# Seven half-size products for the down projection of a SwiGLU half step

## The chip, the cores and the metric

The kernel runs on one core of one Trainium2 chip. The metric is the device time of a whole execution in microseconds; the kernel before takes 1567.97 us (median of three runs, 1567.06 to 1568.4). All data is float32.

## The reference

One layer of a diffusion backbone works on 640 tokens (512 latent, 128 context) of width 1024. It has three parts, each with a modulated RMSNorm ahead of it and a gated residual addition behind it:

```python
def swiglu(h, w_gate, w_up, w_down):
    return (jax.nn.silu(h @ w_gate) * (h @ w_up)) @ w_down

h = modulate(rms_norm(x, norm_ffn1), sh1, sc1)
x = x + 0.5 * gt1 * swiglu(h, w_ffn1_gate, w_ffn1_up, w_ffn1_down)   # first half step
...                                                                  # mixer: Fourier branch and gated linear attention
h = modulate(rms_norm(x, norm_ffn2), sh3, sc3)
x = x + 0.5 * gt3 * swiglu(h, w_ffn2_gate, w_ffn2_up, w_ffn2_down)   # second half step
```

The feed-forward width is 2816, so gate and up map 1024 to 2816 and down maps 2816 back to 1024. The modulation vectors come from a product with `w_ada`, which is streamed in during the first half step.

## The kernel before, in words

**Layout.** Activations stand transposed, with features on the 128 partitions and the 640 tokens along the free axis, cut into two halves of 320 (NH). The 1024 features are 8 tiles of 128, the 2816 hidden features 22 tiles. A "page" is a buffer of 128 x 2 x 640 floats; 26 of them (NPAGES) rotate for everything. Raw weights arrive in two buffers `wraw`, their split copies live in 10 blocks `wspl` (NBLK) of 128 x 2 x 512.

**Precision by splitting.** A float32 value is written as hi + lo, both fp32r: `split` (L105) lets ScalarE copy hi (L107) and VectorE compute lo = src - hi (L108), which reads two operands from SBUF. Every product is then three matmuls: hi*hi, hi*lo, lo*hi.

**Seven products.** `Pair7` (L457) computes two output tiles of 128 features for all 640 tokens as a 2 x 2 block product with seven half-size products in place of eight. With n = 4 inner tiles a product is 4 x 3 = 12 matmuls of 128 x 320 columns, a pair 84. GpSimd forms four sums of the weights in place (L474, L477, L481, L485), all seven weight blocks are split, and class `Take` combines the seven results from PSUM on VectorE (L530 to L545, one ScalarE copy at L529). The sums of the activations are made once, by `Act7`. The products of a pair run in the order 1, 2, 7, 4, 6, 5, 3.

**A half step** (`ffn`, L570). Hidden tiles come in couples f, f+1: a gate pair, then an up pair. `TakeUp.done` multiplies silu(gate) and up on GpSimd (L566, 128 x 640) and splits the result into one page per tile. The 22 tiles are handled in PARTS (4, 6, 6, 6). The down product of a part runs one gate pair late, between the gate and the up pair of the next part: `down` (L587) takes one output tile at a time with plain three-matmul products (L138), 8 x nf x 3 x 2 matmuls for nf hidden tiles, and adds them into X (L372). The last part goes through `halved` (L376): first all eight output tiles for one half of the tokens, then for the other, nf x 3 matmuls each (L392), added to X at L397. While the second half runs, the norm of the first half is already built (first half step: `Norm.add` L319 to L323, `stats` L329, `apply` L355 to L365) or the output is transposed and scaled (second half step: L1267 to L1286). The second half step cuts the tokens at 384 there.

**Start of a half step.** Tiles 0 and 1 are computed with plain products, while `Act7` builds the sums. The order on each engine in that stretch is written out: `pin(m1)` fixes it from `m1 = mark()` on.

**Order.** Outside pinned stretches a planner fixes one order per engine: in its own timing of the program an instruction is placed when its inputs and buffers are there, the earlier line first. At run time each engine's queue, SP's with the weight and `w_ada` loads included, is worked off in that order.

Of the kernel before, what the change touches and what calls it, by code (L numbers as in the profile page):

```python
# [8 lines left out]
F32R = mybir.dt.float32r  # L9
# [6 lines left out]
KD = 8  # L16
# [9 lines left out]
C_F, C_Q, C_K, C_V, C_R, C_A, C_G = 0, 512, 1024, 1536, 2560, 3584, 3616  # L26
NPAGES = 26
NBLK = 10
M1, M2 = 2, 4
PARTS = (4, 6, 6, 6)  # L30


@with_exitstack
def trunk_kernel(ctx: ExitStack, tc: tile.TileContext, I, O):
# [34 lines left out]
    def page(dt=F32):  # L69
        uid[0] += 1  # L70
        return pgs.tile([P, 2, N], dt, tag="pg", name=f"pg{uid[0]}")
# [13 lines left out]
    def out_ps():  # L85
        return [pb_ps(), pb_ps()] if "pb" in ppool else mm_ps()
# [12 lines left out]
    def load(w, r0, nk, c0, cols):  # L99
        uid[0] += 1  # L100
        raw = wraw.tile([P, 2048], F32, tag="wraw", name=f"wraw{uid[0]}")
        v = raw[:, 0:nk * cols].rearrange("p (k c) -> p k c", k=nk)
        SP.dma_start(out=v, in_=w[r0:r0 + nk * P, c0:c0 + cols].rearrange("(k p) c -> p k c", p=P))
        return v

    def split(hi, lo, src, eng=V):
        S.activation(out=hi, in_=src, func=AF.Copy)  # L107
        eng.tensor_tensor(out=lo, in0=src, in1=hi.bitcast(F32), op=ALU.subtract)  # L108
# [51 lines left out]

    # ---------------------------------------------------------------- constants
    ident = const.tile([P, P + 1], F32, name="ident")
# [70 lines left out]

    # ---------------------------------------------------------------- tokens in
    pos = page()
# [67 lines left out]

    # ---------------------------------------------------------------- norm + modulation
    GB = 64
# [3 lines left out]
    class Norm:  # L309
        def __init__(self, stage, full=False):  # L310
            self.stage, self.F = stage, [] if full else None
            self.acc = page()
            self.hs = []
            self.rs = [None, None]
# [52 lines left out]

    # ---------------------------------------------------------------- SwiGLU half step
    def add_gated(ps, gate, X, k, hf):
# [34 lines left out]
    def even(h):  # L404
        return h[:, :, 0:NH]
# [51 lines left out]
    class Pair7:  # L457
        def __init__(self, raw, act, take):
            n = self.n = raw.shape[1] // 2
            self.a11, self.a12, self.a21, self.a22 = [raw[:, k:k + n, c:c + P] for c in (0, P) for k in (0, n)]  # L460
            self.act, self.take = act, take
            self.w, self.p, self.s = {}, {}, set()
# [88 lines left out]
    class TakeGate(Take):  # L551
        tag = "g"

        def done(self, i):
            x = self.x1 if i else self.x0
            S.activation(out=x, in_=x, func=AF.Silu)

    class TakeUp(Take):
        tag = "t"

        def __init__(self, gate, hid):
            self.g, self.hid, self.h = gate, hid, [None, None]

        def done(self, i):
            x, g = (self.x1, self.g.x1) if i else (self.x0, self.g.x0)
            G.tensor_tensor(out=x, in0=x, in1=g, op=ALU.mult)  # L566
            self.h[i] = page(F32R)
            split(self.h[i][:, 0, :], self.h[i][:, 1, :], x)
            if i == 0:
                self.hid += self.h  # L570

    def ffn(hs, F, wg, wu, wd, gate, X, entry, each, mid, parts, fill=lambda: None, first=None, cut=NH):
# [8 lines left out]

        def keep(t, hid):
            h = page(F32R)
            split(h[:, 0, :], h[:, 1, :], t)
            hid.append(h)

        f0 = 0  # L587
        late = []

        def down(f0, nf, hid, take):  # L590
            per = KD // nf * 2
            for m in range(KD):
                if m % per == 0:
                    rd = load(wd, f0 * P, nf, m * P, per * P)
                with tc.issue_after((take.mixed if m < M2 else take.last).ins) if m >= M1 else nullcontext():
                    w = wsplit(rd[:, :, m % per * P:(m % per + 1) * P])
                pd = out_ps()
                gemm_w(pd, w, hid)
                for hf in range(2):
                    add_gated(pd, gate, X, m, hf)  # L600

        for nf in parts:
            hid = []
            for f in range(f0, f0 + nf, 2):
                if f == 0:
# [11 lines left out]
                    act.each(act.sum13)  # L617
                    t = swiglu(p[0], p[1])
                    pair.weights(1)
                    pair.weights(2)  # L620
                    act.each(act.put3)
                    keep(t, hid)
                    pu = out_ps()
# [6 lines left out]
                    pair.weights(4)  # L630
                    t = swiglu(p[2], pu)
                    act.each(act.put2)
                    pair.begin()
                    pair.weights(6)
                    keep(t, hid)
                    act.each(act.put1)
                    pair.weights(5)
                    pin(m1)
# [154 lines left out]

    # ---------------------------------------------------------------- mixer
    psum(True)
# [320 lines left out]

    # ---------------------------------------------------------------- Fourier branch
    dft, four = [], []
# [134 lines left out]

    # ---------------------------------------------------------------- second half step, output
    fng = page().rearrange("p a n -> p (a n)")[:, 0:D]
# [111 lines left out]
```

## Time and profile before

| | us |
|---|---|
| median of three runs | 1567.97 |
| span of the profiled execution, first to last instruction | 1565.3 |
| TensorE busy (share) | 1504.8 (96%) |
| VectorE | 1092.1 (70%) |
| ScalarE | 689.7 (44%) |
| GpSimd | 431.6 (28%) |
| first half step with its entry | about 14 to 522 |
| second half step with its entry | about 1087 to 1565 |

The profile gives no separate time for the profiled execution; its span lies 2.7 us under the median of the runs, which is what lies around it. Times in rows are microseconds from the start of the span. Busy time of VectorE and GpSimd includes time in which an issued instruction is held up.

### The profile page before, as it was taken

The page shows a single profiled execution, that of the slowest core. Times are in us where ns is not written, and L with a number is a line of the kernel's source. Part 1 is how long each engine was busy: PE and PEld are TensorE (multiplying, and loading weights), DVE is VectorE, ACT ScalarE, POOL GpSimd, SP SyncE. Part 2 cuts the span into 40 slices and gives each one's busy share as a digit, 9 for nine tenths or more (in the row PEclk, how much of TensorE's full clock was granted, in tenths as well). Part 3 has the DMA queues.
Part 4 walks back from the last instruction along what each step waited for, and adds up shares of the span by engine and source line. Part 5 has one row for each costly group of instructions (what it writes and reads, how often), then busy time and mean ns, then how long its engine had stood idle before and what let it go on. Part 6 is the DMA issues. An engine that isn't in the chain of part 4 may idle for free.

```text
span 1565.3 us, 27250 instructions
## 1 busy us (share of the span) xinstructions
PE 1504.8 (96%) x10714; PEld 1442.7 (92%) x10714; DVE 1092.1 (70%) x2013; ACT 689.7 (44%) x1397; POOL 431.6 (28%) x320
## 2 busy tenths in 40 slices
PE   7999999999999999999989998989989999999998
PEld 6879989998999899899979998989989999999997
DVE  6866674674577866756768868896787774774676
ACT  5533342342344555454635444344653442442344
POOL 1432521440431000000045424310243432532520
PEclk8999999999999999999999999999999999999999
DMA  9273552454224412213024326354213223222232
GB/s 355 70 255 110 202 169 89 162 175 149 95 88 145 154 54 85 68 45 105 22 74 149 98 92 211 121 182 162 95 55 108 70 78 97 81 79 85 75 102 108
DMA packets 142167, 184.56 MB, mean 118 GB/s; under 512 B 4735, under 2 KB 121847, under 8 KB 142039
## 3 DMA queue, kind: packets, MB, share of 16 engines
q1 hardware_dynamic: 142039, 182.81, 35.3%
q8 instruction: 85, 1.39, 0.4%
q14 instruction: 43, 0.35, 0.1%
HBM read 168.64 MB, written 14.16 MB: 117 GB/s over the span
## 4 chain that ended last, share of the span: by engine, by line
PE 75%; DVE 11%; ACT 4%; issue 4%; DMA 4%; POOL 2%; SPq 0%; POOLq 0%; ACTq 0%; DVEq 0%
PE pb L502 34%; PE pb L138 15%; PE pb L392 7%; PE mm L828 4%; DVE wspl L108 3%; PE mm L138 3%; PE sm L214 2%; PE sc L977 2%; DVE pg L108 2%; DMA pg<-in_w_ada_dram 2%; ACT wspl L107 1%; DMA wraw<-in_w_in_dram 1%; PE sm L828 1%; PE pb L130 1%; PE sm L1007 1%
## 5 line engine op out<-in xcount | busy, mean ns | idle before, releaser
L502 PEld LDWEIGHTS pb<-pg,wspl 128*128 128x128 f32 x4452 | 657.8, 189 | 34.7 <-issue 14.0
L502 PE MATMUL pb<-pg,wspl 128*128 128x320 f32 x4452 | 673.2, 311 | 16.0 <-ACT g L1090 6.3
L108 DVE TENSOR_TENSOR wspl<-wraw,wspl 128x512 fp32r<-128x512 f32 (+1 forms) x619 | 461.7, 762 | 244.3 <-ACT wspl L107 243.5
L107 ACT ACTIVATE wspl<-wraw 128x512 fp32r<-128x512 f32 (+1 forms) x619 | 359.7, 604 | 494.1 <-PE pb L138 165.9
L138 PE MATMUL pb<-pg,wspl 128*128 128x320 f32 x1920 | 289.5, 311 | 5.2 <-DVE pg L1210 5.0
L138 PEld LDWEIGHTS pb<-pg,wspl 128*128 128x128 f32 x1920 | 284.1, 189 | 8.6 <-DVE pg L1210 5.7
L474 POOL TENSOR_TENSOR wraw<-wraw 128x512 f32<-128x512 f32 x53 | 72.5, 1367 | 372.8 <-DVE wspl L108 372.8
L392 PE MATMUL pb<-pg,wspl 128*128 128x320 f32 (+2 forms) x960 | 151.3, 317 | 9.0 <-ACT pg L107 8.4
L392 PEld LDWEIGHTS pb<-pg,wspl 128*128 128x128 f32 x960 | 145.5, 193 | 10.4 <-ACT pg L107 9.3
L481 POOL TENSOR_TENSOR wraw<-wraw 128x512 f32<-128x512 f32 x53 | 69.6, 1313 | 163.3 <-DVE wspl L108 163.3
L108 DVE TENSOR_TENSOR pg<-t,pg 128x640 fp32r<-128x640 f32 (+2 forms) x64 | 60.5, 953 | 39.4 <-ACT pg L107 29.8
L828 PE MATMUL mm<-wspl,pg 128*128 128x256 f32 x672 | 87.8, 286 | 0.1
L107 ACT ACTIVATE pg<-t 128x640 fp32r<-128x640 f32 (+2 forms) x64 | 41.7, 662 | 94.3 <-POOL t L566 85.1
L828 PEld LDWEIGHTS mm<-wspl,pg 128*128 128x128 f32 x672 | 82.4, 191 | 0.7 <-ACT pg L930 0.4
L477 POOL TENSOR_TENSOR wraw<-wraw 128x512 f32<-128x512 f32 x53 | 81.4, 1535 | 4.1
L566 POOL TENSOR_TENSOR t<-t,g 128x640 f32<-128x640 f32 x40 | 64.3, 1618 | 56.7 <-DVE t L540 50.5
L485 POOL TENSOR_TENSOR wraw<-wraw 128x512 f32<-128x512 f32 x53 | 70.7, 1333 | 4.1
L372 DVE SCALAR_TENSOR_TENSOR pg<-pb,hg,pg 128x320 f32<-128x320 f32 x144 | 54.4, 434 | 20.5 <-PE pb L138 20.5
L1029 POOL TENSOR_TENSOR rs<-ms,negh 128x5 f32<-128x5 f32 x4 | 4.8, 1200 | 207.4 <-DVE ms L1027 207.4
L108 DVE TENSOR_TENSOR pg<-pg,pg 128x320 fp32r<-128x320 f32 (+2 forms) x80 | 58.3, 776 | 0.2 <-ACT pg L107 0.2
L138 PE MATMUL mm<-pg,wspl 128*128 128x320 f32 x288 | 52.3, 326 | 0.0
L214 PE MATMUL sm<-pg,cs 128*32 128x256 f32 (+2 forms) x832 | 43.3, 329 | 7.3 <-DMA pg<-in_w_ada_dram 6.5
(211 smaller groups left out, 1524.6 us busy)
## 6 DMA issues: line engine op xcount, KB each, us to landing
pg<-in_w_ada_dram SPq DMA_DIRECT2D x72, 512.0 KB, 6.8
wraw<-in_w_ffn_down_dram SPq DMA_DIRECT2D x32, 768.0 KB, 4.3
wraw<-in_w_ffn_gate_dram SPq DMA_DIRECT2D x22, 1024.0 KB, 5.2
wraw<-in_w_ffn_up_dram SPq DMA_DIRECT2D x22, 1024.0 KB, 5.1
wraw<-in_w_in_dram SPq DMA_DIRECT2D x22, 512.0 KB, 3.8
wraw<-in_w_in_dram SPq DMA_DIRECT2D x10, 1024.0 KB, 5.2
wraw<-in_w_out_dram SPq DMA_DIRECT2D x8, 1024.0 KB, 5.2
gbd<-g SPq DMA_DIRECT2D x16, 320.0 KB, 2.3
```

The costliest lines, as they stand in the source:

```text
L107: S.activation(out=hi, in_=src, func=AF.Copy)
L108: eng.tensor_tensor(out=lo, in0=src, in1=hi.bitcast(F32), op=ALU.subtract)
L138: T.matmul(out=bank(ps, hf)[:, 0:NH], lhsT=w[a][k], rhs=acts[k][:, b, hf * NH:(hf + 1) * NH], start=(k == 0 and ti == 0), stop=(k == nk - ...
L214: T.matmul(out=ps[32 * j:32 * j + 32, 0:nt * 32].rearrange("p (t c) -> p t c", c=32), lhsT=cs[:, k, :], rhs=wv[:, j], start=(k == 0), stop ...
L392: T.matmul(out=ps[:, 0:c1 - c0], lhsT=w[a][i], rhs=acts[i][:, b, c0:c1], start=(i == 0 and ti == 0), stop=(i == nk - 1 and ti == 2))
L474: G.tensor_tensor(out=self.a11, in0=self.a11, in1=self.a21, op=ALU.subtract)
L477: G.tensor_tensor(out=self.a21, in0=self.a21, in1=self.a22, op=ALU.add)
L481: G.tensor_tensor(out=self.a22, in0=self.a22, in1=self.a11, op=ALU.subtract)
L485: G.tensor_tensor(out=self.a12, in0=self.a12, in1=self.a22, op=ALU.subtract)
L502: T.matmul(out=self.p[i], lhsT=self.w[i][:, s, k, :], rhs=x[k][:, t, :], start=(k == 0 and ti == 0), stop=(k == self.n - 1 and ti == 2))
L566: G.tensor_tensor(out=x, in0=x, in1=g, op=ALU.mult)
L828: T.matmul(out=ps_out, lhsT=h2[k][:, a, t * P:(t + 1) * P], rhs=w[b][k], start=(k == 0 and ti == 0), stop=(k == KD - 1 and ti == 2))
```

## The change

PARTS becomes (6, 6, 6, 4). The down product of the first 18 tiles uses `Pair7` with three inner tiles: `alternate=True` takes the even tiles of a part as one row of the 2 x 2 block and the odd ones as the other, so each couple f, f+1 is self-contained. The sums of the hidden activations that this needs are made per couple by the new `Hidden7`, in the up pair's `done` (and in the pinned start for tiles 0 and 1): four GpSimd subtractions of 128 x 320 and seven splits of 128 x 320 in place of two splits of 128 x 640, kept in 3 or 4 pages per couple in place of 2. The results are added to X by `TakeDown`. The last 4 tiles stay plain (`HiddenPlain`, `halved`). Pages go from 26 to 30, blocks from 10 to 9, and the DMA scratch is cut to 1024 bytes.

```diff
-NPAGES = 26
-NBLK = 10
+NPAGES = 30
+NBLK = 9
-PARTS = (4, 6, 6, 6)
+PARTS = (6, 6, 6, 4)
...
-        def __init__(self, raw, act, take):
+        def __init__(self, raw, act, take, alternate=False):
             n = self.n = raw.shape[1] // 2
-            self.a11, self.a12, self.a21, self.a22 = [raw[:, k:k + n, c:c + P] for c in (0, P) for k in (0, n)]
+            ks = (slice(0, 2 * n, 2), slice(1, 2 * n, 2)) if alternate else (slice(0, n), slice(n, 2 * n))
+            self.a11, self.a12, self.a21, self.a22 = [raw[:, k, c:c + P] for c in (0, P) for k in ks]
...
+    class Hidden7:
+        def put(self, where, dst, src):
+            split(dst[:, 0, :], dst[:, 1, :], src)
+            where.append(dst)
+        def second(self, x1):
+            self.h1 = page(F32R)
+            self.put(self.b21, even(self.h1), x1[:, 0:NH])
+            self.put(self.b22, odd(self.h1), x1[:, NH:N])
+        def first(self, x0, x1):
+            h0, pt = page(F32R), page(F32R)
+            f11, f12, f21, f22 = x0[:, 0:NH], x0[:, NH:N], x1[:, 0:NH], x1[:, NH:N]
+            self.put(self.b11, even(h0), f11)
+            G.tensor_tensor(out=f11, in0=f12, in1=f11, op=ALU.subtract)
+            G.tensor_tensor(out=f12, in0=f22, in1=f12, op=ALU.subtract)
+            self.put(self.t1, odd(h0), f11)
+            G.tensor_tensor(out=f22, in0=f22, in1=f11, op=ALU.subtract)
+            self.put(self.t3, odd(pt), f12)
+            G.tensor_tensor(out=f21, in0=f21, in1=f22, op=ALU.subtract)
+            self.put(self.t2, even(pt), f22)
...
+                self.put(self.t4, even(self.p4), f21)
...
+    class TakeDown(Take):
+        def done(self, i):
+            k, x = 2 * self.mp + i, self.x1 if i else self.x0
+            for r, a, b in ((0, 0, NL), (1, NL, N)):
+                V.scalar_tensor_tensor(out=self.X[k][:, a:b], in0=x[:, a:b], scalar=self.gate[:, k, r:r + 1],
+                                       in1=self.X[k][:, a:b], op0=ALU.mult, op1=ALU.add)
...
         def down(f0, nf, hid, take):
...
+            for mp in range(KD // 2):
+                Pair7(load(wd, f0 * P, nf, mp * 256, 256), hid, TakeDown(mp, gate, X), True).run()
...
             # pinned start, tiles 0 and 1
-                    keep(t, hid)
...
-                    keep(t, hid)
+                    hid.second(t1)
                     act.each(act.put1)
+                    hid.first(t0, t1)
                     pair.weights(5)
                     pin(m1)
```

## Rows read from the trace of the kernel before

**Rows 1.** First lines of the page: span, busy time and share of each engine, instructions.
```profile
span 1565.3 us, 27250 instructions
PE 1504.8 (96%) x10714; PEld 1442.7 (92%) x10714; DVE 1092.1 (70%) x2013; ACT 689.7 (44%) x1397; POOL 431.6 (28%) x320
```
**Rows 2.** Stretches: window, length, busy us of engines, clock, DMA share, GB/s.
```profile
150.30:235.80 85.50, 85.18 (x642) 76.90 (x640) 57.94 (x97) 35.04 (x61) 33.87 (x24) 1.00 0.48 170
1238.80:1263.50 24.70, 24.70 (x171) 24.70 (x170) 17.75 (x29) 11.37 (x20) 14.08 (x10) 1.00 0.27 86
1330.30:1404.30 74.00, 74.00 (x507) 74.00 (x506) 55.07 (x90) 32.57 (x59) 33.92 (x24) 1.00 0.24 76
```
**Rows 3.** Timeline, start of the last part, first half step: start, us, engine, line; idle time.
```profile
472.27 2.21 PE L392 MATMUL pb<-pg,wspl 128*128 128x320 f32 x14
476.82 26.14 PE L392 MATMUL pb<-pg,wspl 128*128 128x320 f32 x166 [2.33 <-ACT pg L107]
```
**Rows 4.** The same last part, its second half of the tokens: stretch and timeline.
```profile
497.60:522.20 24.60, 23.74 (x166) 22.85 (x164) 21.41 (x53) 12.44 (x26) 1.17 (x1) 1.00 0.42 134
498.57 0.42 DVE L108 TENSOR_TENSOR wspl<-wraw,wspl 128x256 fp32r<-128x256 f32 x1
522.16 1.55 PE L130 MATMUL mm<-pg,wspl 128*128 128x320 f32 x9 [0.86 <-DVE pg L397]
```
**Rows 5.** Timeline of the last part, second half step, one output tile of either half.
```profile
1520.68 3.37 PE L392 MATMUL pb<-pg,wspl 128*128 128x384 f32 x18
1523.89 0.49 PE L1267 MATMUL pb<-ident,pg 128*128 128x128 f32 x3
1524.13 3.39 PE L392 MATMUL pb<-pg,wspl 128*128 128x384 f32 x18
1540.49 2.39 PE L392 MATMUL pb<-pg,wspl 128*128 128x256 f32 x18
1540.99 0.60 DVE L397 SCALAR_TENSOR_TENSOR pg<-pb,hg,pg 128x128 f32<-128x128 f32 x2
1542.85 2.40 PE L392 MATMUL pb<-pg,wspl 128*128 128x256 f32 x18
1542.86 0.69 DVE L108 TENSOR_TENSOR wspl<-wraw,wspl 128x512 fp32r<-128x512 f32 x1
1543.99 0.48 DVE L1274 TENSOR_TENSOR pg<-pb,pg 128x128 f32<-128x128 f32 x2
```
**Rows 6.** Timeline of VectorE and GpSimd in steady pairs, second half step.
```profile
1253.47 3.10 POOL L566 TENSOR_TENSOR t<-t,g 128x640 f32<-128x640 f32 x2
1255.84 1.41 DVE L108 TENSOR_TENSOR pg<-t,pg 128x640 fp32r<-128x640 f32 x1 [3.10 <-ACT pg L107]
1264.58 0.68 DVE L108 TENSOR_TENSOR wspl<-wraw,wspl 128x512 fp32r<-128x512 f32 x1
1265.34 1.30 POOL L474 TENSOR_TENSOR wraw<-wraw 128x512 f32<-128x512 f32 x1 [3.35 <-DVE wspl L108]
1265.58 0.48 DVE L540 TENSOR_TENSOR g<-sqh,pb 128x320 f32<-128x320 f32 x1
1266.72 1.63 POOL L477 TENSOR_TENSOR wraw<-wraw 128x512 f32<-128x512 f32 x1
1267.51 1.39 DVE L108 TENSOR_TENSOR wspl<-wraw,wspl 128x512 fp32r<-128x512 f32 x1
```
**Rows 7.** Timeline and a stretch of the pinned start, second half step.
```profile
1122.81 0.88 POOL L431 TENSOR_TENSOR pg<-pg 128x320 f32<-128x320 f32 x1 [5.93 <-ACT pg L362]
1136.00:1152.00 16.00, 13.94 (x95) 13.68 (x95) 16.00 (x22) 9.47 (x23) 10.35 (x8) 1.00 0.00 1
1157.16 28.55 PE L502 MATMUL pb<-pg,wspl 128*128 128x320 f32 x190 [0.93 <-DVE wspl L108]
```
**Rows 8.** A long wait of TensorE elsewhere, and the granted clock after it (0.50).
```profile
818.37 13.88 PE L502 MATMUL pb<-pg,wspl 128*128 128x320 f32 x80 [6.28 <-ACT g L1090]
819.00:820.00 1.00, 1.00 (x6) 1.00 (x5) 0.48 (x1) 1.00 (x5) 0.00 (x0) 0.50 0.59 203
```

More of the change, by code (lines that the diff above doesn't have):

```diff
@@ L556, in done, with __init__, one, second @@
             S.activation(out=x, in_=x, func=AF.Silu)
+    class Hidden7:
+        def __init__(self):
+            self.b11, self.b21, self.b22, self.t1, self.t2, self.t3, self.t4 = [[] for _ in range(7)]
+            self.p4 = None
+        def put(self, where, dst, src):
[16 more added lines that the diff above has]
+            self.put(self.t2, even(pt), f22)
+            if self.p4 is None:
+                self.p4 = page(F32R)
+                self.put(self.t4, even(self.p4), f21)
+            else:
+                self.put(self.t4, odd(self.p4), f21)
+                self.p4 = None
+    class HiddenPlain(list):
+        def one(self, x):
+            h = page(F32R)
+            split(h[:, 0, :], h[:, 1, :], x)
+            return h
+        def second(self, x1):
+            self.h1 = self.one(x1)
+        def first(self, x0, x1):
+            self += [self.one(x0), self.h1]
     class TakeUp(Take):
@@ L561, in __init__ @@
         def __init__(self, gate, hid):
-            self.g, self.hid, self.h = gate, hid, [None, None]
+            self.g, self.hid = gate, hid
         def done(self, i):
@@ L566, in done, with __init__ @@
             G.tensor_tensor(out=x, in0=x, in1=g, op=ALU.mult)
[L567 to L570, printed above, removed]
+            if i:
+                self.hid.second(x)
+            else:
+                self.hid.first(x, self.x1)
+    class TakeDown(Take):
+        tag = "t"
+        def __init__(self, mp, gate, X):
+            self.mp, self.gate, self.X = mp, gate, X
+        def done(self, i):
[3 more added lines that the diff above has]
+                                       in1=self.X[k][:, a:b], op0=ALU.mult, op1=ALU.add)
     def ffn(hs, F, wg, wu, wd, gate, X, entry, each, mid, parts, fill=lambda: None, first=None, cut=NH):
@@ L580, in swiglu @@
             return t
[L582 to L585, printed above, removed]
         f0 = 0
@@ L590, in down @@
         def down(f0, nf, hid, take):
[L591 to L600, printed above, removed]
+            for mp in range(KD // 2):
+                Pair7(load(wd, f0 * P, nf, mp * 256, 256), hid, TakeDown(mp, gate, X), True).run()
         for nf in parts:
-            hid = []
+            hid = HiddenPlain() if f0 + nf == DFF // P else Hidden7()
             for f in range(f0, f0 + nf, 2):
@@ L617, in ffn @@
                     act.each(act.sum13)
-                    t = swiglu(p[0], p[1])
+                    t0 = swiglu(p[0], p[1])
                     pair.weights(1)
@@ L630, in ffn @@
                     pair.weights(4)
-                    t = swiglu(p[2], pu)
+                    t1 = swiglu(p[2], pu)
                     act.each(act.put2)
@@ L1347 @@
     from concourse.bass_utils import run_bass_kernel_spmd as _run
-    nc = _bacc.Bacc("TRN2", target_bir_lowering=False, num_devices=1)
+    nc = _bacc.Bacc("TRN2", target_bir_lowering=False, num_devices=1, dynamic_dma_scratch_size=1024)
     arrays, ins, outs = {}, {}, []
```

## Prediction

> **What bounds the kernel now.** I read the page first, then stretches, then the timeline of the stretches that the change touches. TensorE is busy for 96% of the span and no other engine above 70% [rows 1]. In the second half step three couples of hidden tiles fill 74.0 us without a gap, 507 matmuls of 320 columns at 0.146 us each [rows 2]; a couple (gate pair and up pair, 168 matmuls) takes 24.5 us. In the first half step three couples take 85.5 us [rows 2]: 3.9 us more a couple, matmuls of the `w_ada` stream.
>
> Second in line is not an engine but a pair of them. VectorE's lo = src - hi reads two operands from SBUF, and so do GpSimd's sums. The timeline shows that they never run at once. A GpSimd sum runs from 1266.72 to 1268.35; the split that VectorE issued at 1267.51 ends at 1268.90, that is 0.55 us after the sum, where it takes 0.68 us when GpSimd is idle [rows 6]. The 640-wide split ends 0.68 us after the multiplications (1253.47 to 1256.57, split to 1257.25) [rows 6]. The other way round, the sum at 1266.72 takes 1.63 us against 1.30 us [rows 6], because the split ahead of it was still running. A VectorE addition with one operand in PSUM (L540, 0.48 us) runs at its usual speed inside a GpSimd sum [rows 6]. I call what the two share the port. One couple now needs it for 8 sums x 1.30 + 2 multiplications x 1.55 + 14 splits x 0.55 + 2 x 0.68 = 22.6 us, in a couple where TensorE is busy all 24.70 us [rows 2, 6]: 91% full without any harm.
>
> The Trainium skill ("SBUF — State Buffer", section "Who interferes with whom") says this as a rule: a VectorE instruction with two SBUF inputs contends with a GpSimd instruction that reads SBUF, and one of them blocks for the whole instruction. The trace agrees in the 0.55 us above. The rule also covers an operation that the trace does not show against GpSimd, the new addition into X with both operands in SBUF: by it a down pair holds the port 1.4 us longer, 17 us a half step, and without it those 17 us are free.
>
> **The change, part by part.** All of it is per half step unless said otherwise.
>
> *Matmuls.* The downs of the first parts go from 192 + 288 + 288 = 768 matmuls to 3 x 252 = 756: 1.7 us less. The last part goes from 18 to 12 matmuls an output tile and token half, 96 fewer. So nearly all of the gain is in the last part, and it counts only where TensorE is the bound there.
>
> *Last part, first half step.* First token half: 48 matmuls, 7.0 us. But the first tile waits for the last couple's split hidden tiles (2.33 us) after the matmuls of the earlier ones [rows 3]; with 6 of those ahead in place of 12 the wait grows by 0.9 us. Second half: VectorE is busy 21.41 of 24.6 us with the norm of the first half, the additions and the splits, and the matmuls behind wait for it [rows 4]. There I count only what VectorE loses, the second split of each output tile (768 columns become 512): 8 x 0.42 = 3.3 us [rows 4], not the 7.0 us of matmuls. Sum 9.4 us; ends 6 (VectorE gives nothing back) and 14.
>
> *Last part, second half step.* Tiles come every 3.45 us, of which 0.24 us are transposes [rows 5]; two thirds of 3.21 plus 0.24 is 2.38, 1.07 us less, eight times 8.6. Second half: every 2.36 us now; 1.6 us by matmuls, but VectorE needs 0.69 + 0.60 + 0.48 = 1.77 us, some 1.7 back to back [rows 5]; 8 x 0.66 = 5.3 us. Less 1.1 us for the wait at its start: 12.8 us; ends 9 and 14.5.
>
> *Port in the couples.* `Hidden7` adds four subtractions of 128 x 320 (0.88 us each [rows 7]) and seven half-wide splits (0.35 us each, scaled from 0.55 for 512) and drops two of 0.68: +4.6, so 27.2 us of port for 24.5 us of matmuls, in eight couples (tiles 2 to 17). A down pair of 9.2 us of matmuls needs four sums of 384 columns (1.02, between 0.88 and 1.30), seven splits (0.41) and the X additions (1.4): 8.4 us, where the plain downs left the port mostly free. Tiles 2 to 21 with three downs: 8 x 27.2 + 12 x 8.4 + 2 x 22.6 = 363.6 us of port, against 10 x 24.5 + 756 x 0.146 = 355.4 us of matmuls, and 357.1 us before.
>
> How tightly can the port be packed? From below: 91% was reached without being pressed. From above: in the pinned start, with much independent work, 16.0 us hold 8 sums, 4 splits of 512, 15 operations of 320 and one of 640 [rows 7], 16.8 us at the durations above, 105% (two that alternate overlap their starts). In the couples the sums depend on splits in a chain, so I take 99%, between the two: 367.3 us.
> - Second half step: 367.3 - 357.1 = +10.2 us.
> - First half step: the `w_ada` matmuls add 8 x 3.9 = 31 us to TensorE's side (388 before, 386.4 after), more than the port needs. TensorE stays the bound: -1.7 us, and I add 2 us for couples that get fewer of these matmuls.
>
> *Pinned start.* One split of 0.68 us goes from the middle of the stretch. But `pair.weights(5)` now stands behind `hid.first`: five splits interleaved with four subtractions, 3.5 us of GpSimd plus some 2 us of splits at both ends. TensorE waits there 0.93 us already for this weight [rows 7]; the wait would be some 6 us, and after one of 6.28 us the granted clock stood at 0.50, the 1.2 GHz level [rows 8]; at that level 4 us of matmuls cost 2 us more. Behind the waiting copies on ScalarE and VectorE stand the third weight and the next pair's; the pin does not hold those, and their 36 matmuls (5.3 us) could be placed ahead. Ends 0 and 7.5 us; I take 3.5 in the second and 2.5 in the first half step, where the same matmuls share the place with `w_ada` work.
>
> *Costed at nothing.* The weight loads of a down keep their shape and number for six tiles. Nine blocks: a sum of weights at 1265.34 belongs to a pair whose matmuls come more than ten microseconds later, so one block less is within the lead; 3 us if it isn't. Pages: 19 are held by X, h, the sums and the norm, 11 by the hidden tiles of a part, together 30; so from a part's last up pair to the end of its down no page is free for `w_ada`, whose loads SP must issue in order with the weights. The planner can place them elsewhere; 0 to 5 us, part of the 2 us above. The smaller scratch touches no transfer of this kernel.
>
> *Sum.* Second half step: +10.2 - 12.8 + 3.5 = +0.9. First: -1.7 + 2 - 9.4 + 2.5 = -6.6. Together -5.7 us on the span of 1565.3; with the 2.7 us that lie around it, 1568 - 6 = **1562 us**.
>
> **Rivals.**
> *The port does not bind.* If the two engines alternate as in the pinned start (2.5% overlap is enough for 363.6 to fit 355.4), TensorE stays the bound in both half steps: -1.7 - 12.8 + 3.5 - 1.7 - 9.4 + 2.5 = -20: **1548 us**. For it: 105% was seen. Against: there VectorE was never idle [rows 7], while in a couple it is 7 of 24.7 us [rows 2], waiting for copies and matmuls.
> *The port binds hard (slower).* In the couples of the second half step, sums and splits wait for each other in a chain and VectorE, working in order, stands behind a sum while additions from PSUM are due. Filled to 93%, the stretch takes 391 us: +33.9 - 12.8 + 3.5 = +24.6 there, and +3 - 9.4 + 2.5 = -3.9 in the first half step: +21, **1589 us**. It decides below 97.5%, where the sum crosses zero. For it: 91% is all that a couple has shown. Against: nothing pressed it there.
> *Start and pages go wrong.* Both pinned starts at 7.5 us and 2 us more for `w_ada` loads: +11 on the forecast, **1573 us**.
>
> **How the numbers follow.** Forecast (port filled to 96 to 101%, 1554 to 1574): 0.40. Port does not bind (1544 to 1554): 0.24. Port binds hard (1574 to 1610): 0.26. Start and pages (1567 to 1580): 0.10. The median of three runs can't tell less than 0.2%, 3 us, from no change. Faster: 0.24 + 0.23 of the forecast + 0.01 = 0.48; same: 0.11 + 0.03 = 0.14; slower: 0.26 + 0.06 + 0.06 = 0.38. The range 1547 to 1592 leaves out some 0.05 below and 0.1 above; the forecast's own is 1554 to 1574.
>
> **What would show it.** Couples of the second half step: 26 to 28 us by stretches, with TensorE waiting for VectorE's weight splits, against 24.5 if the port does not bind. Downs of six tiles: 37 us. First half step's couples: 28 to 29 us as before. Last part: first token half 7 and 8 us shorter, second half 3 and 5 us. Pinned start: a wait before the fifth product, and, where it is as long as that of [rows 8], the granted clock at 0.50 after it. The prediction is wrong if the couples keep 24.5 us or if a last part shrinks by less than 6 us.

## The result, and the profile after

The changed kernel takes 1727.61 us (median of 4 runs, 1724.79 to 1730.48) against 1567.51 of the kernel before in the same series: 160 us slower, ratio 1.1017 (95% interval 1.1001 to 1.1033). The forecast was 1562 us, its range ended at 1592.

The page of after, beside [rows 1]: TensorE does 216 matmuls less and is busy 89% of the span, VectorE and GpSimd are busy 252 and 187 us longer.

```profile
span 1726.5 us, 27609 instructions
PE 1534.4 (89%) x10498; PEld 1453.0 (84%) x10498; DVE 1343.6 (78%) x2279; ACT 749.6 (43%) x1567; POOL 618.6 (36%) x488
```

Where the 161.2 us of span lie, by stretches. First those of before that the document has not shown: a part of six hidden tiles of the second half step (three couples and a down; from one gate pair to the same gate pair a part later), the products from tile 2 to the start of the last part in the second half step, and the same in the first. Columns as in [rows 2].

```profile
1349.64:1465.80 116.16, 116.16 (x794) 116.16 (x793) 74.01 (x131) 43.00 (x76) 42.03 (x30) 1.00 0.26 82
1142.55:1508.09 365.54, 360.41 (x2451) 359.12 (x2449) 250.50 (x434) 143.69 (x259) 140.27 (x101) 1.00 0.26 83
58.70:472.30 413.60, 407.35 (x2946) 376.91 (x2946) 263.59 (x460) 149.30 (x265) 143.93 (x103) 1.00 0.42 142
```

The same of after; the second line is one down of six tiles, from TensorE's first product of it to the start of the up pair behind it.

```profile
1378.03:1519.55 141.52, 120.07 (x768) 117.47 (x766) 117.94 (x178) 53.84 (x107) 73.20 (x58) 0.95 0.21 68
1444.03:1490.06 46.03, 39.38 (x253) 38.59 (x254) 38.03 (x69) 16.70 (x35) 18.61 (x17) 0.96 0.25 81
1218.34:1677.19 458.85, 386.54 (x2438) 378.33 (x2437) 378.91 (x577) 180.16 (x358) 231.09 (x184) 0.93 0.21 67
57.90:553.40 495.50, 435.64 (x2934) 394.25 (x2933) 389.47 (x605) 184.81 (x365) 236.22 (x186) 0.93 0.35 118
```

The second half step's products take 93.3 us longer, the first's 81.9. The last parts give back 8.7 and 7.9 us (below). The other 2.6 us lie elsewhere. By the starts of TensorE's products the three couples of the steady part take 31.8 us each on average (26.9 to 37.2), where TensorE needs 24.5, and the down takes 46.0, where its 252 matmuls need 36.8. Of the 175 us by which the two stretches grew, TensorE is idle for 121; in the other 54 it is busy longer, with 25 matmuls fewer, and the granted clock there is 0.93, where it was 1.00. Whether the clock costs time of its own, while VectorE and GpSimd are busy nearly throughout (below), no run separates.

What TensorE waits for (waiting engine and line, releaser: us in total, times, longest). Of the first there were 3.1 us before:

```profile
PE pb L503 <- DVE hn L534: 85.6, 31, 6.4
PE sm L214 <- DMA pg<-in_w_ada_dram: 17.0, 12, 4.4
PE pb L503 <- ACT wspl L107: 13.8, 3, 6.2
PE pb L392 <- ACT pg L107: 11.9, 3, 5.5
```

L534 is the addition u += p6. Until it has read its bank, the next product has none to go to. It is short work that is done late. In 30 of the 31 waits the instruction right ahead of it on VectorE is a split of weights, and for 25.1 of the 85.6 us VectorE is idle (counted from the instructions). The timeline around one of these waits, first TensorE, then GpSimd, then VectorE ("..." where lines are left out):

```profile
1444.03 1.58 PE L503 MATMUL pb<-pg,wspl 128*128 128x320 f32 x9 [0.29 <-DVE g L531]
1449.35 2.97 PE L503 MATMUL pb<-pg,wspl 128*128 128x320 f32 x11 [3.74 <-DVE hn L534]
...
1437.19 1.82 POOL L613 TENSOR_TENSOR t<-t,g 128x640 f32<-128x640 f32 x1
1440.12 0.87 POOL L579 TENSOR_TENSOR t<-t 128x320 f32<-128x320 f32 x1 [1.11 <-DVE pg L108]
1441.07 1.07 POOL L580 TENSOR_TENSOR t<-t,t 128x320 f32<-128x320 f32 x1
1442.22 1.01 POOL L582 TENSOR_TENSOR t<-t,t 128x320 f32<-128x320 f32 x1
1443.31 1.00 POOL L584 TENSOR_TENSOR t<-t 128x320 f32<-128x320 f32 x1
1445.95 0.99 POOL L482 TENSOR_TENSOR wraw<-wraw 128x384 f32<-128x384 f32 x1 [1.64 <-DVE wspl L108]
...
1437.50 1.93 DVE L108 TENSOR_TENSOR wspl<-wraw,wspl 128x384 fp32r<-128x384 f32 x1
...
1440.29 1.12 DVE L108 TENSOR_TENSOR wspl<-wraw,wspl 128x384 fp32r<-128x384 f32 x1 [0.24 <-ACT wspl L107]
1441.53 0.96 DVE L108 TENSOR_TENSOR pg<-t,pg 128x320 fp32r<-128x320 f32 x1
1442.68 0.91 DVE L108 TENSOR_TENSOR pg<-t,pg 128x320 fp32r<-128x320 f32 x1 [0.19 <-ACT pg L107]
1443.51 0.47 DVE L531 TENSOR_TENSOR g<-hn,pb 128x320 f32<-128x320 f32 x1
1443.90 0.75 DVE L108 TENSOR_TENSOR pg<-t,pg 128x320 fp32r<-128x320 f32 x1
1444.84 0.49 DVE L108 TENSOR_TENSOR pg<-t,pg 128x320 fp32r<-128x320 f32 x1 [0.19 <-ACT pg L107]
...
1447.53 1.37 DVE L108 TENSOR_TENSOR wspl<-wraw,wspl 128x384 fp32r<-128x384 f32 x2 [1.73 <-ACT wspl L107]
1448.82 0.47 DVE L534 TENSOR_TENSOR hn<-hn,pb 128x320 f32<-128x320 f32 x1
```

Read it by columns of time: while GpSimd subtracts (1440.12 to 1444.31), each split on VectorE is held until a subtraction ends (0.75 to 0.96 us for 320 columns, 0.49 when GpSimd is idle), and L534 comes behind all of them and behind a split that waits for GpSimd's next sum. From here on I also count, from the instructions of a stretch, the time in which VectorE or GpSimd is busy (the union of both). In after's part it is 98%; before, 94% in couples, 60% in a plain down, 81% over the part. My theory after this reading: VectorE and GpSimd are nearly one resource here, whose time adds up, and it is overfull. Rivals: the order on VectorE's queue; the downs alone; the missing block.

### The profile page after: what moved, and what is told of

It reads as the page before. It is cut to its first block, busy times and chain, and to the rows that moved or that the text cites. A ratio compares the mean times of both kernels' runs of the same rounds, so it can differ in the third digit from the quotient of the medians.

```text
span 1726.5 us, 27609 instructions
## 1 busy us (share of the span) xinstructions
PE 1534.4 (89%) x10498; PEld 1453.0 (84%) x10498; DVE 1343.6 (78%) x2279; ACT 749.6 (43%) x1567; POOL 618.6 (36%) x488
## 5 line engine op out<-in xcount | busy, mean ns | idle before, releaser
L503 PE MATMUL pb<-pg,wspl 128*128 128x320 f32 x5964 | 949.7, 321 | 127.4 <-DVE hn L534 85.6
L108 DVE TENSOR_TENSOR wspl<-wraw,wspl 128x512 fp32r<-128x512 f32 (+1 forms) x675 | 566.5, 856 | 200.2 <-ACT wspl L107 198.1
L107 ACT ACTIVATE wspl<-wraw 128x512 fp32r<-128x512 f32 (+1 forms) x675 | 379.7, 597 | 476.1 <-POOL wraw L482 185.0
L475 POOL TENSOR_TENSOR wraw<-wraw 128x512 f32<-128x512 f32 (+1 forms) x77 | 106.2, 1379 | 318.5 <-DVE wspl L108 247.3
L107 ACT ACTIVATE pg<-t 128x320 fp32r<-128x320 f32 (+2 forms) x154 | 72.4, 486 | 199.2 <-POOL t L613 123.7
L108 DVE TENSOR_TENSOR pg<-t,pg 128x320 fp32r<-128x320 f32 (+2 forms) x154 | 137.7, 907 | 21.0 <-ACT pg L107 19.4
L482 POOL TENSOR_TENSOR wraw<-wraw 128x512 f32<-128x512 f32 (+1 forms) x77 | 96.0, 1247 | 135.4 <-DVE wspl L108 135.4
L392 PE MATMUL pb<-pg,wspl 128*128 128x320 f32 (+2 forms) x768 | 124.8, 322 | 12.1 <-ACT pg L107 11.9
L392 PEld LDWEIGHTS pb<-pg,wspl 128*128 128x128 f32 x768 | 118.8, 197 | 13.7 <-ACT pg L107 12.8
L478 POOL TENSOR_TENSOR wraw<-wraw 128x512 f32<-128x512 f32 (+1 forms) x77 | 105.8, 1374 | 5.2
L613 POOL TENSOR_TENSOR t<-t,g 128x640 f32<-128x640 f32 x40 | 68.7, 1718 | 105.2 <-DVE t L541 100.0
L486 POOL TENSOR_TENSOR wraw<-wraw 128x512 f32<-128x512 f32 (+1 forms) x77 | 95.8, 1244 | 5.7
L138 PE MATMUL pb<-pg,wspl 128*128 128x320 f32 x384 | 62.2, 321 | 6.3 <-DVE pg L1256 6.3
L628 DVE SCALAR_TENSOR_TENSOR pg<-t,hg,pg 128x512 f32<-128x512 f32 x96 | 63.0, 694 | 0.0
```

What stands on the lines that cost most here:

```text
L138: T.matmul(out=bank(ps, hf)[:, 0:NH], lhsT=w[a][k], rhs=acts[k][:, b, hf * NH:(hf + 1) * NH], start=(k == 0 and ti == 0), stop=(k == nk - ...
L392: T.matmul(out=ps[:, 0:c1 - c0], lhsT=w[a][i], rhs=acts[i][:, b, c0:c1], start=(i == 0 and ti == 0), stop=(i == nk - 1 and ti == 2))
L475: G.tensor_tensor(out=self.a11, in0=self.a11, in1=self.a21, op=ALU.subtract)
L478: G.tensor_tensor(out=self.a21, in0=self.a21, in1=self.a22, op=ALU.add)
L482: G.tensor_tensor(out=self.a22, in0=self.a22, in1=self.a11, op=ALU.subtract)
L486: G.tensor_tensor(out=self.a12, in0=self.a12, in1=self.a22, op=ALU.subtract)
```

## Experiments

Each run's median time (of two to eight executions), its ratio to before in the same series, and one steady part of six tiles of its second half step, from a gate pair to the same gate pair a part later: length and busy time of the engines in us, and the union.

| run | us | ratio to before (95%) | part | PE | DVE | POOL | DVE or POOL |
|---|---|---|---|---|---|---|---|
| before | 1566 | | 116.2 | 116.2 | 74.0 | 42.0 | 81% |
| after | 1727.6 | 1.102 (1.100 to 1.103) | 141.5 | 120.1 | 117.9 | 73.2 | 98% |
| parts_plain | 1593.3 | 1.017 (1.015 to 1.019) | 120.1 | 118.0 | 83.6 | 44.0 | 82% |
| hidden_only | 1648.8 | 1.053 (1.050 to 1.056) | 129.6 | 121.2 | 92.6 | 54.9 | 85% |
| down_only | 1647.5 | 1.052 (1.049 to 1.055) | 130.4 | 117.4 | 105.6 | 61.9 | 98% |
| subs_vector | 1700.3 | 1.086 (1.082 to 1.089) | 137.9 | 121.3 | 117.6 | 60.5 | 98% |
| parts_26 | 1593.2 | 1.018 (1.014 to 1.022) | 116.2 | 116.2 | 74.0 | 42.0 | 81% |
| down_13 | 1624.2 | 1.038 (1.035 to 1.041) | 122.5 | 115.5 | 93.1 | 61.4 | 96% |
| hidden_late | 1733.7 | 1.108 (1.103 to 1.113) | 147.3 | 120.5 | 107.1 | 72.5 | 96% |
| no_subs | 1669.7 | 1.067 (1.064 to 1.070) | 133.6 | 119.4 | 111.3 | 60.4 | 98% |
| sums_vector | 1604.1 | 1.024 (1.018 to 1.030) | 123.0 | 115.8 | 119.5 | 9.7 | 97% |
| all_vector | 1581.5 | 1.009 (1.007 to 1.012) | 120.2 | 116.2 | 116.6 | 0 | 97% |
| extra_subs | 1606.4 | 1.025 (1.022 to 1.028) | 121.3 | 117.2 | 76.2 | 57.2 | 85% |
| extra_sets | 1567.3 | 1.001 (1.000 to 1.003) | 116.6 | 116.4 | 75.8 | 46.1 | 82% |
| start_five | 1715.8 | 1.095 (1.092 to 1.099) | 141.2 | 120.5 | 117.9 | 73.2 | 98% |
| before_vector | 1549.7 | 0.989 (0.987 to 0.991) | 116.2 | 116.2 | 86.2 | 0 | 74% |
| all_vector_five | 1581.7 | 1.009 (1.006 to 1.011) | 120.1 | 116.1 | 116.6 | 0 | 97% |
| more_sets | 1580.4 | 1.008 (1.006 to 1.011) | 118.8 | 116.4 | 76.6 | 55.6 | 83% |

**Which half of the change costs.** parts_plain is before with the sizes of after:

```diff
-NPAGES = 26
-NBLK = 10
+NPAGES = 30
+NBLK = 9
-PARTS = (4, 6, 6, 6)
+PARTS = (6, 6, 6, 4)
```

> PARTS (6, 6, 6, 4), 30 pages, 9 blocks and the small scratch, but the downs and the hidden tiles as before the change (plain products, two 640-wide splits a couple). Theory (the hidden work of each couple is what costs): nothing of the 160 us is here, the last parts give back their gain of 16 to 22 us: 1546 to 1552 us. Rival (one block less, or pages that keep the w_ada loads back): 1580 us or more. Rival (the plain downs' own gain is nothing): 1566.

Missed, and by an error of mine: with plain products PARTS only moves 96 matmuls (14.1 us) of a half step from the last part into the downs, so there was no gain to expect. It is the zero for the next two, each of which takes one half of the change away:

```diff
 # hidden_only
-                Pair7(load(wd, f0 * P, nf, mp * 256, 256), hid, TakeDown(mp, gate, X), True).run()
...
+                gemm_w(pd, w, hid.pages)
...
 # down_only: Hidden7.first and .second
-            G.tensor_tensor(out=f11, in0=f12, in1=f11, op=ALU.subtract)
...
-                self.put(self.t4, even(self.p4), f21)
...
+            h0 = self.one(x0)
```

> The hidden tiles are split and subtracted as after the change, the downs are plain products again and read the pages as they lie (so the output is not the reference's; the number and shape of matmuls is that of plain downs). Theory (four subtractions and seven splits a couple hold up VectorE and the port): couples stay at 29 to 35 us, the downs go back to some 42 us a part: 1700 to 1725 us. Rival (the downs as seven products are what costs): 1555 to 1575.

> The downs are the seven products of after, with their weight sums and the addition into X, but the hidden tiles are split as before the change, two 640-wide splits a couple and no subtraction (the seven products read these, so the output is not the reference's). Theory (hidden work of the couples): couples 24.5 us in the second half step, downs 38 to 45 us a part: 1550 to 1575 us. Rival (the downs): 1680 or more.

Neither theory nor rival: both halves cost the same, 55 and 54 us over parts_plain, and together (after) 134, 25 more than their sum. My reading, argued and not tested by a run of its own: each alone loads the pair of engines; a plain down leaves it 40% free and repays what the couples overdraw, and with both halves nothing repays.

**Load or chain.** subs_vector moves the four subtractions, no_subs leaves them out:

```diff
-            G.tensor_tensor(out=f11, in0=f12, in1=f11, op=ALU.subtract)
+            V.tensor_tensor(out=f11, in0=f12, in1=f11, op=ALU.subtract)
...
```

> The four subtractions of a hidden couple run on VectorE in place of GpSimd. Theory (VectorE, working in order, stands in a chain subtraction on GpSimd, copy on ScalarE, subtraction on VectorE, and the additions that free PSUM banks stand behind): the chain loses its slowest links, 1600 to 1665 us. Rival (only the amount of time on the port counts, at the packing of 0.83 that the couples show): 27.2 to some 25.6 us a couple, 1.9 us less for each of 16 couples: 1695 us. Rival (VectorE itself is full): 1740 or more.

> The four subtractions of a hidden couple are left out, their splits stay (so the output is not the reference's). Port a couple 27.2 - 3.5 = 23.7 us. Theory (chain): the links through GpSimd go, the splits follow each other without a wait: 1660 to 1685 us, as down_only plus the splits. Rival (port at a packing of 0.83): 4.2 us less for each of 16 couples: 1660 as well; told from the chain by subs_vector, which took 1.6 us of port and won 27 us. Rival (the splits and the nine blocks are what costs): 1700 or more.

There are 72 of them (18 couples). At 0.88 us each [rows 7] they are 63 us; without them the kernel is 57.9 us faster. On VectorE one takes 0.49 us, 0.41 from start to start, so moving them saves 34 us of the two engines' time; the kernel is 27.3 us faster. Both are eight to nine tenths of the load, and the chain's reading of subs_vector (1600 to 1665) is wrong. (no_subs by itself doesn't tell the two apart: both had it near 1660.) hidden_late keeps the load and changes the order of the hidden work:

```diff
+        def step(self, ins):
+            if steps:
+                with tc.issue_after(ins.ins):
+                    steps.pop(0)()
...
+        def uv(self, p6, p7):
+            super().uv(p6, p7)
+            self.step(self.mixed)
```

> The same work as after the change, on the same engines, but the subtractions and the four splits that follow from them are cut in four steps and put on VectorE's queue behind the additions c11, uv, c22 and c12 of the next gate pair, instead of right behind the up pair. Theory (VectorE stands in the chain while the additions that free PSUM banks are due): 30 to 60 us come back, 1665 to 1700 us. Rival (the amount of port time): within 10 us of 1727. Rival (the temporaries of the up pair are held longer and hold up the next pair): slower than 1737.

1733.7 us: nothing comes back, and TensorE still waits for L534 31 times (93.9 us). But the edit did not bring that addition forward. One of these waits, TensorE, then GpSimd, then VectorE:

```profile
1384.79 27.47 PE L503 MATMUL pb<-pg,wspl 128*128 128x320 f32 x168 [7.35 <-DVE hn L534]
...
1378.01 1.26 POOL L482 TENSOR_TENSOR wraw<-wraw 128x512 f32<-128x512 f32 x1
1379.23 0.86 POOL L609 TENSOR_TENSOR t<-t,t 128x320 f32<-128x320 f32 x1
...
1379.97 0.69 DVE L108 TENSOR_TENSOR wspl<-wraw,wspl 128x512 fp32r<-128x512 f32 x1 [3.59 <-ACT wspl L107]
1383.64 0.69 DVE L108 TENSOR_TENSOR wspl<-wraw,wspl 128x512 fp32r<-128x512 f32 x1 [2.99 <-ACT wspl L107]
1384.25 0.48 DVE L534 TENSOR_TENSOR hn<-hn,pb 128x320 f32<-128x320 f32 x1
```

Two splits of weights still stand ahead of it. They wait for copies that come behind GpSimd's sums of weights, with the subtractions now between these sums, and VectorE is idle for 6.6 us. A split of weights stands right ahead of L534 in all 31 waits, and VectorE is idle in 43.9 of their 93.9 us. So the place of the hidden work is not the cause; whether an L534 ahead of the weight splits would win time, no run tests.

**Blocks.** parts_26 is before with PARTS alone, down_13 has 13 blocks:

```diff
 # parts_26, against parts_plain            # down_13, against down_only
-NPAGES = 30                                -NPAGES = 30
-NBLK = 9                                   -NBLK = 9
+NPAGES = 26                                +NPAGES = 26
+NBLK = 10                                  +NBLK = 13
```

> PARTS (6, 6, 6, 4) alone, with 26 pages and 10 blocks; all products plain as before. My expectation for the run before this one forgot that 96 plain matmuls of a half step (14.1 us) move from the last part into the downs: with plain products the number of matmuls is that of before, and the last part gives back some 8 us only. So PARTS alone is worth +10 to +16 us. Theory (one block less holds up the weights of a couple, 27.9 us there against 25.6): couples at 25.6 us, 1578 to 1583 us. Rival (the blocks do nothing, it is PARTS and the order that follows from it): 1590 to 1596.

> down_only again (seven-product downs, hidden tiles split as before the change; output not the reference's) with 26 pages and 13 blocks in place of 30 and 9. A part of the second half step takes 130.4 us there, against 110.9 of matmuls. Rival (blocks: a down pair takes seven of nine, and the copies into the next ones wait): a part falls to 111 to 116 us, 1560 to 1580 us in all. Theory (chain of sums and splits between GpSimd, ScalarE and VectorE, with the additions that free PSUM banks behind it): only the 3.9 us a part that parts_plain shows too come back, 1615 to 1635.

The tenth block does bring the steady part back to 116.2 us, but the time stays at 1593, the rival's value: the second half step's products win 5.8 us and the first's lose as much. So PARTS alone costs 28 us here, where I had 10 to 16; the rest isn't traced. (With fewer pages the `w_ada` stream waits longer, 8.7 against 5.1 us; that this is all of it isn't shown.) In the seven-product downs blocks count: 7.9 us a part, between theory and rival, and 23 us in all, which is in the theory's range. (With 13 blocks more of the additions from PSUM lie beside a GpSimd operation: 14.4 of 31.8 us a part, 4.5 in down_only, counted from the instructions.)

**GpSimd's work on VectorE.** If the two are one resource, what is dear on GpSimd should move: a sum of 512 columns takes 1.30 us there [rows 6]. sums_vector moves the four sums of `Pair7` and the subtractions, all_vector also the multiplication:

```diff
-                G.tensor_tensor(out=self.a11, in0=self.a11, in1=self.a21, op=ALU.subtract)
+                V.tensor_tensor(out=self.a11, in0=self.a11, in1=self.a21, op=ALU.subtract)
...
-            G.tensor_tensor(out=x, in0=x, in1=g, op=ALU.mult)
+            V.tensor_tensor(out=x, in0=x, in1=g, op=ALU.mult)
```

> As after the change, with all sums of weights in Pair7 (four a pair) and the four subtractions of a hidden couple on VectorE; the multiplication silu(gate) x up stays on GpSimd. What no_subs and subs_vector point to: in the slow stretches VectorE or GpSimd is busy 97 to 98% of the time, so each microsecond of either counts in full (3.5 us less a couple gave 57.9 us in all, 1.7 us less gave 27.3). Theory (the two engines together are one resource): a sum of 512 columns costs 0.55 on VectorE in place of 1.30 on GpSimd, 6.0 us a couple and 2.4 us a down pair less than subs_vector, together 16 x 6.0 + 24 x 2.4 + 4 x 6.0 = 178 us, more than TensorE's matmuls leave: TensorE is the bound again in most stretches, 1555 to 1610 us. Rival (VectorE in order is what holds up TensorE, and it gets more work): 1700 or more.

> As sums_vector, and the multiplication silu(gate) x up on VectorE too: GpSimd does nothing in the couples and the downs. Theory (two engines, one resource): another 2 x (1.55 - 0.69) = 1.7 us a couple less, 24.1 us of VectorE for 24.5 of matmuls: 0 to 25 us faster than sums_vector. Rival (GpSimd beside VectorE is worth something, an operation there runs beside the additions from PSUM): slower than sums_vector by 10 us or more.

Both as the theory had them: 1604.1 and 1581.5 us, 146 us back with GpSimd idle in the products. Groups of VectorE's instructions (busy us, mean ns) in one part of all_vector, and of after:

```profile
L108 DVE TENSOR_TENSOR wspl<-wraw,wspl 128x512 fp32r<-128x512 f32 x42 | 27.8, 687 | 0.6 <-ACT wspl L107 0.5
L475 DVE TENSOR_TENSOR wraw<-wraw 128x512 f32<-128x512 f32 x6 | 4.1, 685 | 0.0
L534 DVE TENSOR_TENSOR hn<-hn,pb 128x320 f32<-128x320 f32 x10 | 4.9, 486 | 0.5 <-PE pb L503 0.2
```
```profile
L108 DVE TENSOR_TENSOR wspl<-wraw,wspl 128x512 fp32r<-128x512 f32 x42 | 40.9, 988 | 12.7 <-ACT wspl L107 12.4
L108 DVE TENSOR_TENSOR pg<-t,pg 128x320 fp32r<-128x320 f32 x21 | 21.0, 1009 | 2.6 <-ACT pg L107 2.4
L534 DVE TENSOR_TENSOR hn<-hn,pb 128x320 f32<-128x320 f32 x10 | 4.7, 474 | 0.0
```

The same 42 splits take 40.9 us beside GpSimd and 27.8 without, and VectorE's idle time for copies goes from 12.4 to 0.5 us. The addition from PSUM is the same in both: it is not held, it only stands behind what is. In all_vector VectorE is the bound, 97% busy, so the seven-product downs, 31.5 us of matmuls less, still don't pay.

**The port by itself.** Four subtractions, and then memsets, that nobody waits for, added to before behind the two multiplications of a couple:

```diff
             mul = G.tensor_tensor(out=x, in0=x, in1=g, op=ALU.mult)
+            for _ in range(2):                      # more_sets: 6
+              with tc.issue_after(mul.ins):
+                G.tensor_tensor(out=dm[:, 0], in0=dm[:, 0], in1=dm[:, 1], op=ALU.subtract)
+                                                    # extra_sets, more_sets: G.memset(dm[:, 0], 0.0)
```

> The kernel before the change with four more GpSimd subtractions of 128 x 320 a couple, on a tile that nothing else reads or writes, two behind each multiplication silu(gate) x up (the small DMA scratch makes room for the tile). They are in no chain: they take GpSimd and, reading SBUF, the port. 3.5 us a couple, 26.1 us of port for 24.5 us of matmuls. By my forecast's rule (additions from PSUM are free, port filled to 99%): 26.4 us a couple, +1.9 in the second half step, nothing in the first: 1585 us. Theory (VectorE and GpSimd together are the resource, 95% full in a couple already): 28 us a couple or more in both half steps, 1600 to 1635 us. Rival (it was the chain of sums and splits, not the load): 1568 to 1575.

> The control for extra_subs: the same places on GpSimd's queue, but a memset of the same 128 x 320 tile, which reads nothing from SBUF. If it is the shared port that makes the two engines one resource, VectorE runs beside these and the time stays within 8 us of before. If it is GpSimd's own queue (the sums behind come late), it goes up with the memsets' own duration, as in extra_subs.

> extra_sets with twelve memsets of 128 x 320 a couple in place of four: 12 x 0.36 = 4.4 us of GpSimd a couple, as much as the four subtractions of extra_subs took (12 in 14.1 us, 4.7 us a couple), but with no read of SBUF. Theory (it is the port, held by what reads SBUF on both engines): within 8 us of before, 1565 to 1574. Rival (GpSimd's queue: the sums of weights behind come late): 1590 to 1606, as extra_subs.

extra_subs costs 40.8 us, where the forecast's rule gave 19: no chain is needed. The same GpSimd time in memsets (13.1 us in 36, against 14.1 us in 12 subtractions, in 120 us) costs 12.3 us, and four a couple 1.6. So more_sets lies between theory and rival: by these two times about a third comes with GpSimd's queue, the rest with the reads. Its timeline, GpSimd then VectorE:

```profile
1353.94 2.90 POOL L571 MEMSET dm<- 128x320 f32 x7
1354.80 0.83 DVE L108 TENSOR_TENSOR pg<-t,pg 128x640 fp32r<-128x640 f32 x1 [0.26 <-ACT pg L107]
1355.65 0.69 DVE L108 TENSOR_TENSOR wspl<-wraw,wspl 128x512 fp32r<-128x512 f32 x1
```

Two splits run inside the memsets at full speed. The Trainium skill ("SBUF — State Buffer", section "Who interferes with whom") has it so: such a VectorE instruction contends with a GpSimd instruction that reads SBUF, not with one that only writes it; these 0.83 and 0.69 us agree.

**The pinned start, and before itself.**

```diff
 # start_five, all_vector_five
+                    pair.weights(5)
                     hid.first(t0, t1)
-                    pair.weights(5)
```

> As after the change, but in the pinned start the fifth weight of the first pair stands ahead of the hidden splits and subtractions of tiles 0 and 1, as before the change. After shows a wait of 6.19 us there in the second half step and a like one in the first. Theory (two engines, one resource, full for the tens of us that follow): the wait goes, but the work that stood ahead now stands behind, and most of it comes back in the next couples: 1718 to 1726 us. Rival (the start's wait is a cost of its own): 1711 to 1716 us, 12 us and more less than 1727.6.

> all_vector with the fifth weight ahead of the hidden work in the pinned start. Theory (VectorE is 97% busy after the start as well, so what leaves the start comes back behind): 1574 to 1581 us. Rival (the start's wait of 5.3 us is a cost of its own, twice): 1569 to 1572. Neither reaches the 1566 of before.

start_five wins 11.9 us, the rival's value: in after the two starts' waits are a cost of their own. In all_vector the same edit wins nothing. before_vector makes all_vector's edits (sums and multiplication) in the kernel before:

> The kernel before the change with the four sums of weights of every pair and the multiplication silu(gate) x up on VectorE in place of GpSimd. Theory (VectorE and GpSimd share their time; 0.6 to 0.7 us of each sum is saved): couples are at TensorE's limit already (24.5 us), so only the starts of the half steps and the mixer's pairs gain: 1552 to 1564 us. Rival (VectorE, in order, has no room left at 21 to 22 of 24.5 us a couple): 1570 to 1590.

1549.7 us, 16.5 us faster than before (1566.24), just under the theory's range, and the one version here that beats both kernels. Its part is at TensorE's limit, as before's:

```profile
1349.64:1465.80 116.16, 116.16 (x795) 116.16 (x794) 86.17 (x161) 44.55 (x76) 0.00 (x0) 1.00 0.26 82
```

The gain lies at the seams. The span is 15.8 us shorter: 3.1 us in the first half step's products, 3.5 in its last part and the entry of the mixer, 3.6 at the projection into the second half step, 2.4 in the last part of the second, the rest in the mixer's pairs and the second start.

## Why the prediction was wrong, point by point

**The step that failed** is "How tightly can the port be packed?", where I took 99% of 115.2 us of port a part (3 x 27.2 + 4 x 8.4). Measured: 141.5 us. Two things are in it.

First the durations. A split of 512 columns was put at 0.55 us, what it still takes after a sum ends [rows 6]. Alone it is 0.69 us, 0.60 from start to start; the 320-wide one 0.49 and 0.41, not 0.35. With after's own figures: GpSimd 6 x 1.55 + 24 x 1.30 + 16 x 1.01 + 12 x 0.88 = 67.2 us a part. VectorE's own time is all_vector's 116.6 less the 58 operations that moved there (36.2 us busy, 31.6 at 0.08 us of overlap each): 85.0. Of it 70 additions from PSUM x 0.40 are 28. So the port's time was 67.2 + 57.0 = 124.2 us, not 115.2. (The additions into X, which no trace of before could show against GpSimd, do contend: one of 128 columns takes 1.21 us on average beside a GpSimd operation in after, 0.34 alone.)

Second, and more: I let all 28 us of additions from PSUM run beside GpSimd for nothing, since one does so in [rows 6]. They can, but VectorE works in order and mostly stands in a held split or waits for GpSimd's result when GpSimd runs. Own times add up to 152.2 us, the part took 141.5. Counted from the instructions, the additions' records fill 31.8 us of it, and only 5.8 of these lie beside a GpSimd operation. By the same sum no_subs has 141.6 us (took 133.6) and subs_vector 146.6 (137.9), 94% of it where after takes 93%. The share is no constant: down_only and down_13 both have 137.5 us and took 130.4 (95%) with nine blocks and 122.5 (89%) with 13, and hidden_only has 122.4 and took 129.6. How much overlaps depends on the blocks too, and no run gives after itself more of them. For before the sum is 40.5 + 67.1 = 107.6 us (67.1: before_vector's 86.2 less the moved work) under TensorE's 116.2: that is why a port "91% full" did no harm. Its couples need 13.5 + 15.5 = 29.0 us of the two engines in 24.5 us of TensorE and live on what the plain downs leave: in [rows 2] three couples hold 24 of their 30 GpSimd operations, and the other six lie beside the plain down. I took a couple that borrows for one that fits.

**First half step.** "TensorE stays the bound", for the 31 us of `w_ada` matmuls, failed with it: +81.9 us in place of +2.8 with the start (in the second half step +93.3 in place of +13.7). 31 us of cover are less than half of 25 us a part in three parts. TensorE also waited 17.0 us for `w_ada` loads, 6.5 before, for which I had 0 to 5.

**Rivals.** "Binds hard" named the mechanism, VectorE in order behind sums while additions from PSUM are due, but gave it 93% of the wrong total and kept the first half step out: 1589 us. The load half is shown by the runs that change the load; of its order half hidden_late rules out the place of the hidden work, and the place of the weight splits is not tested.

**Matmuls and last parts.** The count was right (216 less). The last part's matmuls run from 553.42 to 594.66 in the first half step, 41.2 us against 49.9 [rows 3, 4]: -8.7, forecast -9.4. That is close by luck: the first token half is 4.4 us shorter (forecast 6.1), the second 4.3 (forecast 3.3). In the second half step the tail from 1677.19 is 49.3 us against 57.2: -7.9, forecast -12.8 and under its lower end of 9. The wait at its start was mis-sized: 5.50 us, 2.27 before, where I allowed 1.1 more. TensorE, after:

```profile
553.42 2.36 PE L392 MATMUL pb<-pg,wspl 128*128 128x320 f32 x15
594.66 4.22 PE L130 MATMUL mm<-pg,wspl 128*128 128x320 f32 x18 [3.27 <-DVE pg L397]
...
1677.19 2.27 PE L392 MATMUL pb<-pg,wspl 128*128 128x384 f32 x12
1684.96 4.18 PE L392 MATMUL pb<-pg,wspl 128*128 128x384 f32 x12 [5.50 <-ACT pg L107]
```

**Pinned start.** Right in place and kind. The wait before the fifth product is 6.19 us (forecast some 6), and the granted clock stands at 0.50, the 1.2 GHz level, after it (timeline of TensorE, then a stretch, the clock third from the end):

```profile
1237.19 25.10 PE L503 MATMUL pb<-pg,wspl 128*128 128x320 f32 x156 [6.19 <-ACT wspl L107]
```
```profile
1238.00:1239.00 1.00, 1.00 (x6) 0.99 (x5) 1.00 (x3) 0.70 (x2) 0.00 (x0) 0.50 0.00 0
```

start_five prices both at 11.9 us; I took 6, with ends at 0 and 15. The lower clock I had costed here alone; it follows the longer waits of the couples and downs as well.

**What would show it.** I named couples of 26 to 28 us with TensorE waiting for weight splits: they are 26 to 37 us by TensorE's products, and it waits for a PSUM bank. **Costed at nothing:** one block less costs 3.9 us in parts_plain's part (25.9 us a couple on average, 24.6 in parts_26) though not in its time, and more where the downs need seven blocks a pair (down_13).

What stays open: how much of the overlap lost is the port, how much VectorE's waiting on GpSimd's results, and how much the order that puts L534 behind weight splits; no run separates them in after itself.

## What to carry to other kernels

Where VectorE works on two SBUF operands, GpSimd beside it is hardly a second engine: add both engines' own times over a stretch and compare with TensorE's (where that sum was the larger, parts here took 89 to 106% of it), and count additions from PSUM as VectorE's time, not as free. Take the sum over the whole cycle, with the stage that repays the lead, and price an operation by its unhindered duration, not by what is left of it after a hold. When the sum is near the limit, try the work on VectorE alone before building anything on top.

## What the runs showed of the hardware

A two-operand fp32 operation from SBUF takes about twice as long on GpSimd as on VectorE: 1.30 against 0.69 us at 128 x 512, 0.88 against 0.49 at 320, 1.55 against 0.82 at 640. (The Trainium skill, "GPSIMD Engine Reference", section "4.1 Engine selection", says about half VectorE's speed for two inputs; these agree.) GpSimd's memset of 128 x 320 took 0.36 us; the 41 splits of 512 and 640 columns that ran beside memsets alone in more_sets took their usual 0.69 and 0.82 us on average. And the clock also fell after a shorter wait than that of [rows 8]: behind the 3.74 us in which TensorE waited for L534 above, it was at 0.50:

```profile
1450.00:1451.00 1.00, 1.00 (x5) 1.00 (x5) 0.96 (x3) 0.00 (x0) 0.00 (x0) 0.50 0.09 26
```
